# A decoder layer on one core: transpositions written into the out-projection's row parts, a gain row spread first on TensorE, and the last sums of one gate block held back

## The chip, the core and the metric

The kernel runs on one core of a Trainium2 chip, in one launch. The metric is device time in microseconds. TensorE is called PE in the profile, and its weight loads PEld; VectorE is DVE, ScalarE is ACT, GpSimd is POOL and SyncE is SP. Every matrix product of the layer is done in three PE passes over a number that has been split into a high and a low part, so "H" and "L" at the end of a tile's name are the two halves of one operand.

## The reference

One layer of a hybrid decoder on 1024 tokens of width 1024, in float32:

```
h = rms_norm(x, norm_mix)
proj = h @ w_in                      # 1024 x 8192: xa, ga, q, f, v, g, m_a, m_b
y_a = rg_lru(conv(xa)) * gelu(ga)
y_b = rms_norm(hgrn2(silu(q), f, v), hg_norm) * silu(g)
y = sigmoid(m_a) * y_a + sigmoid(m_b) * y_b
x = x + y @ w_out                    # out-projection
h = rms_norm(x, norm_mlp)
x = x + square(relu(h @ w_up)) @ w_down
out = rms_norm(x, norm_final)
```

## The kernel before

**Stages.** The tokens are worked in two halves of 512 (`c` = 0, 1), each half in four row tiles of 128 tokens. In order of time: `first_norm` brings in the first four row tiles, normalises and transposes them; eight stages of projections and recurrences follow (to about 560 us); then the gate products (`gate_step`, `gate_work`); then the out-projection, for the first half in `out_proj(0, ...)` and for the second half in a loop over two "row parts" of two row tiles each; then the MLP's first product (`product`, `hidden`) and its second one, with the final norm at the end.

**What sets the order.** A scheduler orders each engine's instructions by priority and by its own estimate of when an operand is ready, except where `keep` or `pin` record that an instruction stays in the order of the source (`pin` only while `pinned[0]` is true), where `add_manual_dep(..., NoSync, ...)` puts one instruction behind another on the same engine, or where `high_priority` lifts it.

**The start.** `first_norm` (L281 on) loads x, weights, and the 1 x 1024 row of the first norm's gain (`gain_row`, on ACT's DMA queue). The gain is spread over 128 partitions by two matmuls of a row of ones (written by POOL, L298) with that row (L305), into two PSUM banks (`spread`). PE also runs transposes of an identity matrix into a bank that nobody reads (`idle`): five ahead of the two matmuls (L302) and seven behind them (L307). ACT copies the two halves of the spread gain to SBUF (L335), DVE scales the first row tile by them (L328), PE transposes it (L178), ACT casts the high half (`hT00H`, L87), and the first projection (`pv`) begins.

**The gates.** There are sixteen gate blocks `q`; block q % 4 says which of the four gate kinds it is, and the four blocks of a channel pair are combined into `y`. Blocks 0 and 1 were made earlier, so `own` is the list 2 to 15: `own[0]` = 2, `own[1]` = 3, `own[2]` = 4. A block has seven products of 12 matmuls each (steps 0 to 6 of `PLAN`, a Strassen-like scheme); steps 0, 2, 4 and 6 add into one bank X. Steps 0, 1 and 2 are copied out by ACT; steps 3, 4 and 5 are added up by DVE (L1071); step 6 is copied out by ACT (L1073). Step 6 adds on to the bank that step 4's DVE addition reads. In the profile a block's operands carry its number plus 32: `wA1236` is step 3's and 6's weight of block 4. `gate_work(3)` finishes the first `y`: a product with g1 (L1121), four sums with g2 (L1124), and the split into `yH` (ACT) and `yL` (DVE). It stands in the source behind all seven steps of block 3, as every block's work does. The block's first product and the next block's are placed by the scheduler there.

**The out-projection.** `out_proj(0, ...)` runs 192 matmuls (8 weight tiles x 2 x 4 row tiles x 3 passes) and adds x (L929). `second_norm(tt, 0)` for the four row tiles then does: sum of squares on ACT (L165), rstd on DVE and POOL (L166, L171), scaling on DVE (L172), eight PE transposes into two "hg" banks (L1268), a copy of each bank by ACT (L1269) and the split of it. The row parts (`for part in range(2)`) follow: each has two halves `hf` of the output columns, each half four weight tiles `j`, each of them 12 matmuls (2 x 2 row tiles x 3 passes) in the bank `po`. The transposes of the first half's four tiles (`xT_h`) have been issued in the source ahead of this loop, and those of the second half's tiles at the end of their row part; where they stand on PE among the loop's matmuls is the scheduler's choice, since `pinned[0]` is set only in the last quarter (part 1, hf 1). `second_norm(tt, 1)` ends in `operands()`, a generator of the MLP's combined operands (t1, B22, n2, T3, T4), on DVE and ACT, run by `rest_of_it`.

Of the kernel before, what the change touches and what calls it, by code (L numbers as in the profile page):

```python
# [18 lines left out]
P = 128  # L19
# [26 lines left out]
def trunk(ctx: ExitStack, tc: tile.TileContext, x, wts, mlp, pv, gains, mask_f, mask_u, out):  # L46
# [236 lines left out]
    def first_norm():  # L283
        dst = hT[0]
        halves = (slice(0, D // 2), slice(D // 2, D))
        xts = []
        for tt in range(4):
            xt = mt(X_TAGS[tt], f"x{tt}", (P, D))
            for cols in halves if tt == 0 else (slice(0, D),):
                nc.sync.dma_start(xt[:, cols], x[tt * P : (tt + 1) * P, cols])  # L290
            xts.append(xt)
            if tt < 2:
                raws.append(load_w(tt))
        raws.append(load_w(2))
        line = mt("qb", "gain_row", (P, 1792))
        row, ones = line[0:1, 0:D], line[0:1, D : D + P]
        nc.scalar.dma_start(row, gains[0:1, :])
        G.memset(ones, 1.0)  # L298
        gain0.append(const.tile([P, D], F32, tag="gain", name="gain0", bufs=1))
        idle = bank("sc", "idle")  # L300
        for _ in range(5):
            keep(PE.transpose(idle[:, :P], ident, ident))  # L302
        spread = [bank("pj", f"gain{h}") for h in range(2)]
        for h, cols in enumerate(halves):
            keep(PE.matmul(spread[h], ones, row[:, cols], start=True, stop=True))  # L305
        for _ in range(7):
            keep(PE.transpose(idle[:, :P], ident, ident))  # L307
        xns, rs = {}, {}

        def squares(tt):  # L310
            xn = xns[tt] = mt("f" if tt % 2 == 0 else "tmp", f"xn0{tt}", (P, D))
            r = rs[tt] = const.tile([P, 1], F32, tag="rstd", name=f"rstd_x0{tt}", bufs=4)
            if tt:
                keep(A.activation(xn, xts[tt], AF.Square, scale=D**-0.5, accum_out=r))
                keep(V.tensor_scalar(r, r, EPS, None, op0=ALU.add))
            else:
                two = const.tile([P, 2], F32, tag="ossq", name="first_sq", bufs=8)
                for h, cols in enumerate(halves):
                    keep(A.activation(xn[:, cols], xts[tt][:, cols], AF.Square, scale=D**-0.5, accum_out=two[:, h : h + 1]))
                keep(V.tensor_tensor(out=r, in0=two[:, 0:1], in1=two[:, 1:2], op=ALU.add))  # L320
                keep(V.tensor_scalar(r, r, EPS, None, op0=ALU.add))
            keep(G.tensor_tensor(out=r, in0=r, in1=mhalf[:, 0:1], op=ALU.pow))

        def scaled(tt):
            for h, cols in enumerate(halves) if tt == 0 else ((0, slice(0, D)),):
                g = gain0[0][:, cols] if tt else spread[h]
                keep(
                    V.scalar_tensor_tensor(  # L328
                        xns[tt][:, cols], xts[tt][:, cols], rs[tt][:, 0:1], g, op0=ALU.mult, op1=ALU.mult
                    )  # L330
                )

        squares(0)
        for h, cols in enumerate(halves):
            keep(A.copy(gain0[0][:, cols], spread[h]))  # L335
        scaled(0)
        fill_w(1)
        squares(1)
        for tt in range(4):
            transposed(xns[tt], dst, tt, f"x0{tt}")  # L340
            if tt < 3:
                scaled(tt + 1)
                if tt < 2:
                    squares(tt + 2)
                if tt == 0:
                    fill_w(2)
        fill_w(3)
        in_order[0] = False
# [735 lines left out]
    def gate_work(q):  # L1084
# [28 lines left out]
        else:  # L1113
# [3 lines left out]
            for c in range(NC):  # L1117
                two = slice(2 * c, 2 * c + 2)
                for j in (2 * c, 2 * c + 1):
                    A.activation(b[:, j, :], b[:, j, :], AF.Sigmoid, scale=SIGN[j])  # L1120
                V.tensor_tensor(out=b[:, two, :], in0=b[:, two, :], in1=g1[:, two, :], op=ALU.mult)  # L1121
                for j in (2 * c, 2 * c + 1):
                    op = ALU.add if p == 0 or SIGN[j] > 0 else ALU.subtract
                    V.tensor_tensor(out=b[:, j, :], in0=b[:, j, :], in1=g2[:, j, :], op=op)  # L1124
                if last and c == 0:
                    split(b[:, two, :], yt[0][p][:, 0], yt[0][p][:, 1])
                else:
                    split(b[:, two, :], yh[:, two, :], yl[:, two, :])
                    for t, y in enumerate((yh, yl)):
                        nc.sync.dma_start(yd[p][:, t, two, :], y[:, two, :].bitcast(F32))  # L1130
# [51 lines left out]
    for q in own:  # L1182
# [3 lines left out]
        for step in (1, 2, 5, 4, 6) if q == own[0] else (0, 1, 2, 3, 4, 5, 6):  # L1186
# [3 lines left out]
            gate_step(q, step)  # L1190
            if q == own[0] and step == 4:
                gate_step(own[1], 0)
            if q == own[1] and step == 6:
                pinned[0] = False
                gate_step(own[2], 0)
                with_o(0)
                gate_work(own[0])
# [13 lines left out]
            for k in {2: ("sums", "a", "b"), 5: ("c",), 6: ("d",)}.get(step, ()):  # L1211
                if q > own[0]:
                    gwork[n][k]()
                elif k != "a":
                    with tc.high_priority(300):
                        gwork[n][k]()
        if q > own[0]:
            gate_work(q)
    close_gp()
    close_tp()  # L1220
# [32 lines left out]
    def second_norm(tt, half):  # L1253
# [8 lines left out]
        def op_split(src, o):  # L1262
            return split(src.rearrange("p (k t) -> p k t", k=4), hop[o][0][:, :, cut], hop[o][1][:, :, cut])

        for h in range(2):
            pt = bank("hg", f"xT_h{t}_{h}")
            for k in range(4):
                pin(PE.transpose(pt[:, k * P : (k + 1) * P], xn[:, (4 * h + k) * P : (4 * h + k + 1) * P], ident))  # L1268
            A.copy(b[:, h, :], pt)  # L1269
            if half == 0:  # L1270
                op_split(b[:, h, :], ("B11", "B21")[h])

        def operands():
            b0 = braw[tt, 0]
# [18 lines left out]
            op_split(b21, "T4")  # L1293
            yield

        return operands()

    rest, t1_ops, n2_ops = [], [], []

# [26 lines left out]
                work[0]["sums"]()  # L1326
                work[0]["b"]()

    for tt in range(4):
        second_norm(tt, 0)  # L1330
    close_rows()
    homes("B22")
    for part in range(2):
        tts = (2 * part, 2 * part + 1)
        for tt in tts:
# [2 lines left out]
        for hf in range(2):  # L1338
            pp = {tt: bank("pj", f"po1{hf}{tt}") for tt in tts}
            turn = [(j, tts) for j in range(4)]  # L1340
            if (part, hf) == (1, 1):
                turn = turn[:2] + [(j, tts[i : i + 1]) for i in range(2) for j in (2, 3)]
                pinned[0] = True
            for n, (j, those) in enumerate(turn):
                if n == 4:
                    first_weights()
                wh, wl = out_w[4 * hf + j]
                for k in range(2):
                    ku = 2 * j + k
                    yh, yl = ykt1(part, ku)  # L1350
                    cols = slice(k * 512, (k + 1) * 512)
                    for tt in those:
                        cut = slice((tt % 2) * P, (tt % 2 + 1) * P)
                        mm3(pp[tt], yh[:, cut], yl[:, cut], wh[:, cols], wl[:, cols], ku == 0, ku == 7)
            for tt in tts:
                cols = slice(hf * 512, (hf + 1) * 512)
                V.tensor_tensor(out=x2s[tt][:, cols], in0=pp[tt], in1=x2s[tt][:, cols], op=ALU.add)
        for i, tt in enumerate(tts):
            if part:
                product(i, 0)  # L1360
            nc.sync.dma_start(x2d[4 + tt], x2s[tt])
            rest.append(second_norm(tt, 1))
    with tc.high_priority(400):
        work[0]["d"]()
    product(0, 3)
# [270 lines left out]
```

## Time and profile before

| | us |
|---|---|
| runs: median of 3 | 1549.08 |
| runs: lowest, highest | 1548.0, 1550.54 |
| the profiled execution's own time | 1550.47 |
| its span, first to last instruction | 1548.7 |
| PE busy | 1528.6 (99%) |
| PEld busy | 1274.5 (82%) |
| DVE busy | 1151.0 (74%) |
| ACT busy | 809.3 (52%) |
| POOL busy | 154.5 (10%) |

A line of the timeline gives start, duration, engine, source line, operation, output<-inputs, shapes and a count where neighbours of one kind were merged; a bracket at its end gives how long the engine had been idle before it, and what ended that. A line of the waits gives who waited for whom, the total, how often, and the longest. Matmuls are pipelined: the time from one start to the next is what one costs, and it is shorter than the duration shown.

### The profile page before, as it was taken

What the parts mean: (1) busy time and instruction counts of PE and PEld (TensorE: products, weight loads), DVE (VectorE), ACT (ScalarE), POOL (GpSimd) and SP (SyncE); (2) the same over time, 40 slices, a digit from 0 to 9 for tenths busy, and PEclk for the clock granted to TensorE, in tenths of its full rate; (3) what the DMA queues carried; (4) which work ended last, traced back from release to release, by engine and by line L of the source; (5) the groups of instructions that cost most, each with busy time, mean ns of one, the idle gap of its engine ahead of it and who ended that gap; (6) DMA issues with size and microseconds to landing.
All of it is one profiled execution on the core that took longest, in us unless ns stands there. A gap on an engine that the chain in (4) does not pass through costs nothing. (4 is left out here: it accounts for less than half of the span.)

```text
span 1548.7 us, 23204 instructions
## 1 busy us (share of the span) xinstructions
PE 1528.6 (99%) x9088; PEld 1274.5 (82%) x9088; DVE 1151.0 (74%) x1656; ACT 809.3 (52%) x1341; POOL 154.5 (10%) x188
## 2 busy tenths in 40 slices
PE   9999999999999999999999999999999999999998
PEld 7878888888888887888888778888888788888886
DVE  5798695485675838786856568888888898888877
ACT  5656757567567335454533347766776721111115
POOL 1022210232614600000000000000000000000000
PEclk9999999999999999999999999999999999999999
DMA  8545455465674275332339223666666675666642
GB/s 295 191 158 191 150 192 195 150 215 173 222 229 140 99 295 187 126 136 82 136 107 333 117 109 141 268 246 250 248 251 247 220 307 215 253 250 251 253 187 109
DMA packets 81679, 306.82 MB, mean 198 GB/s; under 512 B 8481, under 2 KB 20897, under 8 KB 68642
## 3 DMA queue, kind: packets, MB, share of 16 engines
q1 hardware_dynamic: 77536, 292.75, 51.5%
q10 hardware_dynamic: 4034, 12.59, 2.1%
q8 instruction: 71, 1.16, 0.3%
q14 instruction: 38, 0.31, 0.1%
HBM read 201.50 MB, written 103.81 MB: 197 GB/s over the span
## 5 line engine op out<-in xcount | busy, mean ns | idle before, releaser
L1545 DVE TENSOR_TENSOR acc<-acc,dX 128x512 f32<-128x512 f32 x128 | 85.2, 685 | 28.8 <-PE dX L146 27.2
L87 ACT CAST wA<-q 128x512 fp32r<-128x512 f32 x46 | 28.6, 622 | 148.3 <-PE dX L146 102.4
L88 DVE TENSOR_TENSOR wL<-raw,wH 128x1024 fp32r<-128x1024 f32 x48 | 58.9, 1226 | 43.1 <-ACT wH L87 42.8
L87 ACT CAST wH<-raw 128x1024 fp32r<-128x1024 f32 x48 | 50.4, 1050 | 36.7 <-DMA raw<-wts_in 14.5
L1545 DVE TENSOR_TENSOR acc<-acc,dY 128x512 f32<-128x512 f32 x64 | 43.5, 686 | 13.1 <-PE dY L146 12.9
L145 PE MATMUL po<-wL,y 128*128 128x512 f32 x128 | 50.0, 391 | 0.0
L146 PE MATMUL po<-wH,y 128*128 128x512 f32 x128 | 49.9, 391 | 0.0
L144 PE MATMUL po<-wH,y 128*128 128x512 f32 x128 | 49.5, 390 | 0.0
L1406 ACT ACTIVATE b<-b 128x512 f32<-128x512 f32 x48 | 30.2, 630 | 32.7 <-DVE b L1405 32.5
L88 DVE TENSOR_TENSOR wA<-q,wA 128x512 fp32r<-128x512 f32 x46 | 31.5, 687 | 19.0 <-ACT wA L87 18.9
L108 ACT CAST wH<-raw 128x1024 fp32r<-128x1024 f32 x36 | 37.7, 1048 | 9.7 <-issue 3.7
L171 POOL TENSOR_TENSOR rstd_h<-rstd_h,mhalf 128x1 f32<-128x1 f32 x8 | 4.6, 585 | 376.1 <-DVE rstd_h L166 376.1
L465 DVE SCALAR_TENSOR_TENSOR xc<-xp,pvt,xc 128x512 f32<-128x512 f32 x48 | 40.1, 846 | 1.1 <-ACT xc L449 1.1
L981 DVE TENSOR_TENSOR s<-q,q 128x512 f32<-128x512 f32 x46 | 31.6, 688 | 5.3 <-DMA q<-mlp_in 5.0
L378 POOL TENSOR_TENSOR stt<-r,stt 128x256 fp32r<-128x256 f32 x16 | 19.8, 1261 | 127.4 <-ACT stt L377 115.3
L989 DVE TENSOR_TENSOR s<-q 128x512 f32<-128x512 f32 x46 | 31.6, 687 | 0.4
L1407 ACT ACTIVATE b<-b 128x512 f32<-128x512 f32 x48 | 30.2, 631 | 1.2
L769 ACT ACTIVATE on<-po 128x128 f32<-128x128 f32 x64 | 16.9, 278 | 26.1 <-PE po L765 26.0
L144 PEld LDWEIGHTS po<-wH,y 128*128 128x128 f32 x128 | 24.0, 188 | 4.9
L145 PEld LDWEIGHTS po<-wL,y 128*128 128x128 f32 x128 | 24.0, 188 | 4.9
L146 PEld LDWEIGHTS po<-wH,y 128*128 128x128 f32 x128 | 24.0, 188 | 4.8
L1071 DVE TENSOR_TENSOR gb<-gY,ge 128x512 f32<-128x512 f32 x14 | 9.7, 691 | 24.1 <-PE gY L146 24.1
(2548 smaller groups left out, 5453.6 us busy)
## 6 DMA issues: line engine op xcount, KB each, us to landing
q<-mlp_in SPq DMA_DIRECT2D x92, 512.0 KB, 3.7
raw<-wts_in SPq DMA_DIRECT2D x80, 512.0 KB, 4.8
rest<-wL SPq DMA_DIRECT2D x36, 512.0 KB, 2.9
wL<-rest SPq DMA_DIRECT2D x36, 512.0 KB, 4.1
hd<-ri SPq DMA_DIRECT2D x16, 256.0 KB, 3.8
od<-onT ACTq DMA_DIRECT2D x8, 512.0 KB, 7.1
cdT<-stT SPq DMA_DIRECT2D x16, 256.0 KB, 3.2
o<-od SPq DMA_DIRECT2D x4, 1024.0 KB, 7.4
```

Source lines behind the costliest of these rows:

```text
L87: keep(A.copy(h, src))
L88: ins = V.tensor_tensor(out=lo, in0=src, in1=h.bitcast(F32), op=ALU.subtract)
L108: A.copy(h, raw)
L144: pin(PE.matmul(o, ah, bh, start=first, stop=False, **how))
L145: pin(PE.matmul(o, ah, bl, start=False, stop=False, **how))
L146: pin(PE.matmul(o, al, bh, start=False, stop=last, **how))
L465: ins = V.scalar_tensor_tensor(xc[:, s, :], xp[:, j : j + T], pvt[:, PV_CW + 8 * j + u : PV_CW + 8 * j + u + 1], xc[:, s, :], op0=ALU.mult ...
L981: ins = V.tensor_tensor(out=sa[:, 0, :], in0=a21, in1=a22, op=ALU.add)
L989: V.tensor_tensor(out=sb[:, 0, :], in0=a21, in1=a11, op=ALU.add)
L1406: A.activation(b[:, at, :], b[:, at, :], AF.Relu, scale=-1.0 if at == 2 else 1.0)
L1407: A.activation(b[:, at, :], b[:, at, :], AF.Square)
L1545: V.tensor_tensor(out=dst, in0=dst, in1=banks[bk, pr], op=op)
```

## The change

Three places are edited.

**Start.** The five idle transposes ahead of the two gain matmuls go, and of the seven behind them five stay. On PE the program began, before:

```order
L302 MATMUL idle<-ident 128x128 x5
L305 MATMUL gain_156<-gain_row 128x512
L305 MATMUL gain_157<-gain_row 128x512
L307 MATMUL idle<-ident 128x128 x7
L178 MATMUL xT_x_0_190<-ident,xn_167 128x128 x4
L178 MATMUL xT_x_1_197<-ident,xn_167 128x128 x4
```

and begins now:

```order
L305 MATMUL gain_151<-gain_row 128x512
L305 MATMUL gain_152<-gain_row 128x512
L307 MATMUL idle<-ident 128x128 x5
L178 MATMUL xT_x_0_183<-ident,xn_160 128x128 x4
L178 MATMUL xT_x_1_190<-ident,xn_160 128x128 x4
```

The gain matmuls are now PE's first instructions. They no longer stand behind the identity matrix.

**Gates.** `gate_work(3)` is issued after step 4 of block 4 instead of after block 3, and its sums L1124 get an order (no semaphore) behind block 4's step-4 addition. On DVE, around the end of the first `y` (`gb_6351` is block 3's sum, `gb_6487` is block 4's), before:

```order
L88 TENSOR_TENSOR ws137L<-s_6573,ws137H 128x1024
L1121 TENSOR_TENSOR gb_6351<-gb_6351,gb_6246 128x1024 x2
L1124 TENSOR_TENSOR gb_6351<-gb_6351,g_0_6279 128x512 x4
L88 TENSOR_TENSOR yL_6521<-gb_6351,yH_6520 128x1024
L1071 TENSOR_TENSOR gb_6487<-gZ_6586,ge_4_6500 128x512
L1071 TENSOR_TENSOR gb_6487<-gX_6486,ge_4_6553 128x512
```

and now (`gb_6344` is block 3's, `gb_6480` is block 4's):

```order
L88 TENSOR_TENSOR ws137L<-s_6546,ws137H 128x1024
L1071 TENSOR_TENSOR gb_6480<-gZ_6559,ge_4_6493 128x512
L1121 TENSOR_TENSOR gb_6344<-gb_6344,gb_6239 128x1024 x2
L1071 TENSOR_TENSOR gb_6480<-gX_6479,ge_4_6526 128x512
L1124 TENSOR_TENSOR gb_6344<-gb_6344,g_0_6272 128x512 x4
L1071 TENSOR_TENSOR gb_6480<-gY_6513,ge_4_6544 128x512
L88 TENSOR_TENSOR yL_6587<-gb_6344,yH_6586 128x1024 x2
```

Block 4's three additions now stand between and ahead of block 3's last sums. On PE the 12 matmuls of block 4's step 6 (`gX<-gT4H,wA1236H` and its fellows) stood behind the 12 of block 5's step 0 and one of its step 1; now they stand ahead of them. The split `wA` of block 6's first weight moves a few places back on DVE, and on SP one weight load (`q<-mlp_in`) moves ahead of the load `o<-od`.

**Out-projection.** In `second_norm` the transposes with their copies and splits become a function `turned()` that the caller runs. The four of the first half are run after chosen weight tiles of part 0 (hf 0 after the second, third and fourth; hf 1 after the first), those of part 0's own tiles after the second and third of part 1, and those of part 1's tiles where they were. `pinned[0]` is true from the start of the loop. On PE, around the first of these transposes, before (11 matmuls of part 0 stand ahead):

```order
L145 MATMUL po_8538<-wL_8051,y_8150 128x512
L146 MATMUL po_8538<-wH_8050,y_8150 128x512
L144 MATMUL po_8539<-wH_8050,y_8150 128x512
L145 MATMUL po_8539<-wL_8051,y_8150 128x512
L1268 MATMUL xT_h_0_8446<-ident,xn_h_8440 128x128 x4
L1268 MATMUL xT_h_1_8454<-ident,xn_h_8440 128x128 x4
L146 MATMUL po_8539<-wH_8050,y_8150 128x512
L144 MATMUL po_8538<-wH_8096,y_8151 128x512
L145 MATMUL po_8538<-wL_8097,y_8151 128x512
L1268 MATMUL xT_h_0_8468<-ident,xn_h_8462 128x128 x4
```

and now (24 matmuls of part 0 stand ahead, and 12 between each two groups of transposes):

```order
L144 MATMUL po_8468<-wH_8089,y_8144 128x512
L145 MATMUL po_8468<-wL_8090,y_8144 128x512
L146 MATMUL po_8468<-wH_8089,y_8144 128x512
L1274 MATMUL xT_h_0_8493<-ident,xn_h_8433 128x128 x4
L1274 MATMUL xT_h_1_8501<-ident,xn_h_8433 128x128 x4
L144 MATMUL po_8467<-wH_8095,y_8145 128x512
L145 MATMUL po_8467<-wL_8096,y_8145 128x512
L146 MATMUL po_8467<-wH_8095,y_8145 128x512
```

The groups of the first half stood after 11, 14, 18 and 22 matmuls of the loop and stand now after 24, 36, 48 and 60; the two of part 0's tiles move from 13 and 15 matmuls into part 1 to 24 and 36. Before, several groups split a row of three passes.

The diff:

```diff
@@ first_norm
-        for _ in range(5):
+        for _ in range(0):
             keep(PE.transpose(idle[:, :P], ident, ident))
         spread = [bank("pj", f"gain{h}") for h in range(2)]
         for h, cols in enumerate(halves):
             keep(PE.matmul(spread[h], ones, row[:, cols], start=True, stop=True))
-        for _ in range(7):
+        for _ in range(5):
             keep(PE.transpose(idle[:, :P], ident, ident))
@@ gate_work
                     op = ALU.add if p == 0 or SIGN[j] > 0 else ALU.subtract
-                    V.tensor_tensor(out=b[:, j, :], in0=b[:, j, :], in1=g2[:, j, :], op=op)
+                    ins = V.tensor_tensor(out=b[:, j, :], in0=b[:, j, :], in1=g2[:, j, :], op=op)
+                    if q == own[1]:
+                        how = mybir.DependencyInfo(mybir.DependencyClass.NoSync, mybir.DependencyReason.DATA)
+                        tc.add_manual_dep(ins.ins, added[own[2], 4].ins.name, how, reason="sums of the next")
@@ the loop over the blocks
+            if q == own[2] and step == 4:
+                gate_work(own[1])
...
-        if q > own[0]:
+        if q > own[1]:
             gate_work(q)
@@ second_norm
-        for h in range(2):
-            pt = bank("hg", f"xT_h{t}_{h}")
-            for k in range(4):
-                pin(PE.transpose(pt[:, k * P : (k + 1) * P], xn[:, (4 * h + k) * P : (4 * h + k + 1) * P], ident))
-            A.copy(b[:, h, :], pt)
-            if half == 0:
-                op_split(b[:, h, :], ("B11", "B21")[h])
+        def turned():
+            for h in range(2):
+                pt = bank("hg", f"xT_h{t}_{h}")
+                for k in range(4):
+                    pin(PE.transpose(pt[:, k * P : (k + 1) * P], xn[:, (4 * h + k) * P : (4 * h + k + 1) * P], ident))
+                A.copy(b[:, h, :], pt)
+                if half == 0:
+                    op_split(b[:, h, :], ("B11", "B21")[h])
...
-        return operands()
+        return turned, operands()
@@ the row parts
-    for tt in range(4):
-        second_norm(tt, 0)
+    turns = {}
+    for tt, at in enumerate(((0, 0, 1), (0, 0, 2), (0, 0, 3), (0, 1, 0))):
+        turns[at], _ = second_norm(tt, 0)
     close_rows()
     homes("B22")
+    pinned[0] = True
...
             if (part, hf) == (1, 1):
                 turn = turn[:2] + [(j, tts[i : i + 1]) for i in range(2) for j in (2, 3)]
-                pinned[0] = True
...
+                if (part, hf, n) in turns:
+                    turns.pop((part, hf, n))()
...
-            rest.append(second_norm(tt, 1))
+            turn, ops = second_norm(tt, 1)
+            rest.append(ops)
+            if part:
+                turn()
+            else:
+                turns[1, 0, i + 1] = turn
```

## The prediction

> **What bounds the kernel now.** I read the page first, then the waits by PE, then the timeline at each edited place. The page says that PE is the bound:
>
> ```profile
> PE 1528.6 (99%) x9088; PEld 1274.5 (82%) x9088; DVE 1151.0 (74%) x1656; ACT 809.3 (52%) x1341; POOL 154.5 (10%) x188
> ```
>
> PE does the same products after the change, so only its stalls can be won: the span of 1548.7 us less 1528.6 busy leaves 20.1 us, much of which is the short gap at each change of operands. The waits by PE name the larger stalls of which the change speaks:
>
> ```profile
> PE gX L144 <- DVE gb L1071: 1.2, 1, 1.2
> PE xT_h L1268 <- DVE xn_h L172: 0.9, 2, 0.5
> PE xT_h L1268 <- ACT ws10H L87: 0.7, 1, 0.7
> PE xT_h L1268 <- ACT h2B11H L87: 0.6, 1, 0.6
> PE xT_h L1268 <- DVE rstd_h L166: 0.3, 1, 0.3
> ```
>
> The first is a gate product; the other four lines are five stalls at the transposes of the out-projection. The idle time understates a stall, since PE is still shown busy while its pipeline drains; I count from start to start below. The first ten microseconds are a third place: there PE is shown busy with transposes that nobody reads.
>
> **The out-projection.** Two neighbours give the normal step; then come the five stalled groups, the last start before the fourth group, the start of part 1, and the scaling of the fourth row tile:
>
> ```profile
> 872.59 0.39 PE L144 MATMUL po<-wH,y 128*128 128x512 f32 x1
> 872.82 0.39 PE L145 MATMUL po<-wL,y 128*128 128x512 f32 x1
> 873.51 1.09 PE L1268 MATMUL xT_h<-ident,xn_h 128*128 128x128 f32 x8 [0.30 <-DVE rstd_h L166]
> ...
> 875.62 1.06 PE L1268 MATMUL xT_h<-ident,xn_h 128*128 128x128 f32 x8 [0.32 <-DVE xn_h L172]
> ...
> 879.01 0.39 PE L144 MATMUL po<-wH,y 128*128 128x512 f32 x1
> 880.03 1.06 PE L1268 MATMUL xT_h<-ident,xn_h 128*128 128x128 f32 x8 [0.62 <-ACT h2B11H L87]
> ```
>
> ```profile
> 897.76 0.39 PE L144 MATMUL po<-wH,y 128*128 128x512 f32 x1
> ...
> 901.55 1.06 PE L1268 MATMUL xT_h<-ident,xn_h 128*128 128x128 f32 x8 [0.68 <-ACT ws10H L87]
> ...
> 903.62 1.06 PE L1268 MATMUL xT_h<-ident,xn_h 128*128 128x128 f32 x8 [0.54 <-DVE xn_h L172]
> ```
>
> A step is 0.23 us. From 872.82 to 873.51 is 0.69, so the first stall costs 0.46 with an idle of 0.30: the drain adds 0.16 to each. The fourth group: 880.03 - 879.01 - 0.23 = 0.79, again 0.17 over its idle of 0.62. The five together: idle 0.30 + 0.32 + 0.62 + 0.68 + 0.54 = 2.46, plus 5 x 0.16 = 3.3 us.
>
> Is the operand there at the new places? The eleventh matmul of the loop starts at 872.82, so the first did at 872.82 - 10 x 0.23 = 870.5. With 24 ahead the first group comes at 870.5 + 5.5 = 876.0; its rows were used at 873.51, a margin of 2.5 us. Each next group comes 12 steps and a group later, 2.75 + 0.9: 879.7, 883.3, 887.0; before, the second came at 875.62 and the fourth at 880.03. The two banks are free long before, since ACT takes 0.59 for such a copy (in the start's rows below), 1.2 for a group's two, and there are 2.75 between groups. In part 1, from 897.76 on, the groups come at 903.3 and 907.0 on the old clock, against 901.55 and 903.62. So all five stalls go. The new pins add nothing by themselves: `po` matmuls stood in that order before, only with groups pushed in among them. Bounds: 3.3 is all there is, plus nothing; at the low end I leave half a stall, 0.4, at each of the two groups of part 1, whose ACT queue now has two weight casts ahead of the copies: 2.5. I take **3.3**.
>
> What is late next is DVE's work behind the second pair's transposes; one weight split in it, its end, and what follows:
>
> ```profile
> 903.39 1.22 DVE L88 TENSOR_TENSOR ws10L<-s,ws10H 128x1024 fp32r<-128x1024 f32 x1
> ...
> 917.17 0.69 DVE L1290 SCALAR_TENSOR_TENSOR xn_h<-xn_h,xn_h 128x512 f32<-128x512 f32 x1
> 920.40 0.69 DVE L1357 TENSOR_TENSOR x2s<-po,x2s 128x512 f32<-128x512 f32 x1 [2.53 <-PE po L146]
> ```
>
> It has 2.53 us to spare ahead of the last sums of the out-projection, which PE brings 3.3 us earlier; the queue of DVE itself starts 1.7 earlier (the first three stalls, 0.46 + 0.48 + 0.79). So 2.53 - (3.3 - 1.7) = 0.9 us remain, if DVE finds other work while it waits for the later groups; three weight splits of 1.2 us each (`ws10L`, `wA120L`, `ws30L`) are there for it.
>
> **The gate block.** PE at block 5's step 0 and at the stall, then DVE:
>
> ```profile
> 613.36 0.39 PE L144 MATMUL gX<-hT00H,wA 128*128 128x512 f32 x1
> ...
> 616.08 0.39 PE L144 MATMUL gY<-gt1H,ws137H 128*128 128x512 f32 x1
> 617.66 0.50 PE L144 MATMUL gX<-gT4H,wA1236H 128*128 128x512 f32 x1 [1.20 <-DVE gb L1071]
> ```
>
> ```profile
> 610.45 2.36 DVE L1121 TENSOR_TENSOR gb<-gb,gb 128x1024 f32<-128x1024 f32 x2
> 612.72 2.50 DVE L1124 TENSOR_TENSOR gb<-gb,g 128x512 f32<-128x512 f32 x4
> 615.18 1.23 DVE L88 TENSOR_TENSOR yL<-gb,yH 128x1024 fp32r<-128x1024 f32 x1
> 616.33 0.68 DVE L1071 TENSOR_TENSOR gb<-gZ,ge 128x512 f32<-128x512 f32 x1
> 616.93 0.68 DVE L1071 TENSOR_TENSOR gb<-gX,ge 128x512 f32<-128x512 f32 x1
> ```
>
> The stall is 617.66 - 616.08 - 0.23 = 1.35 us: step 6 adds on to the bank that the last addition shown reads, and DVE reaches it only at 616.93 because the sums and one split stand ahead. Now DVE goes from 610.45: addition of gZ (616.93 - 616.33 = 0.60 a step) to 611.05, the two products (612.72 - 610.45 = 2.27) to 613.32, addition of gX done at 613.32 + 0.68 = 614.00. PE, which has step 6 next instead of step 0 of block 5, is ready at 613.36 and starts at 614.05: a stall of 0.7 remains, **0.7** is won. That the sums are held costs DVE nothing, since it has the same instructions; the sums start 613.92 - 612.72 = 1.2 us later and the splits `yL` follow. Behind them wait the stores of y and, on SP, the load `o<-od` into the same buffer; block 5's work reads it after that block's 84 products, 84 x 0.23 = 19 us of cover. The weight load moved ahead of it on SP is for block 7, which is still further off; without that cover a late o or weight would cost PE its lateness one to one. Bounds: 0 if DVE is held elsewhere and PE then stalls as long at the earlier place, 1.35 if the order leaves no stall.
>
> **The start.**
>
> ```profile
> q10 hardware_dynamic: 2, 0.00, 0.5%
> ```
>
> ```profile
> 2.26 0.20 POOL L298 MEMSET gain_row<- 1x128 f32 x1
> ...
> 2.37 1.33 PE L302 MATMUL idle<-ident 128*128 128x128 f32 x5 [2.37 <-POOL ident masks.py:199]
> ...
> 3.63 3.78 PE L305 MATMUL gain<-gain_row 1*128 1x512 f32 x4
> ...
> 7.33 1.76 PE L307 MATMUL idle<-ident 128*128 128x128 f32 x7
> 7.44 0.59 ACT L335 COPY gain<-gain 128x512 f32<-128x512 f32 x1 [1.12 <-PE gain L305]
> ...
> 8.06 0.75 DVE L328 SCALAR_TENSOR_TENSOR xn<-x,rstd_x,gain 128x512 f32<-128x512 f32 x1 [0.62 <-ACT gain L335]
> ...
> 8.87 1.06 ACT L314 ACTIVATE xn<-x 128x1024 f32<-128x1024 f32 x1
> 8.88 1.91 PE L178 MATMUL xT_x<-ident,xn 128*128 128x128 f32 x8
> ...
> 9.98 0.59 ACT L87 CAST hT00H<-xT_x 128x512 fp32r<-128x512 f32 x1
> ...
> 10.62 0.58 PE L144 MATMUL pv<-wH,hT00H 128*128 128x256 f32 x1
> ...
> 13.68 1.03 PE L178 MATMUL xT_x<-ident,xn 128*128 128x128 f32 x8
> ```
>
> The first line is from the DMA view of the first 2 us: both packets of ACT's queue, the gain row and its signal, are through by then. The ones are written at 2.46, so the gain matmuls can start at 2.5 instead of 3.63: 1.1 us. They end at 6.3; the five idle transposes (0.25 each) at 7.5; the second half of the first tile, which waited 0.62 for the copy, is scaled from 7.44 on. Transposes run from 7.5 instead of 8.88. On ACT the squares of the next tile stand ahead of `hT00H`:
>
> ```profile
> L290 SPq DMA_DIRECT2D x<-x_in x1: 432/432/432, 2.1 to 2.1; - x1
> ...
> DMA to landing us min/median/max: 5.8/5.8/5.8
> ```
>
> That tile lands at 2.1 + 5.8 = 7.9, so the squares move from 8.87 to no earlier than 7.9, and the cast from 9.98 to about 9.1. I take **0.9**, which the rest of the start (same engines, same order, the same queue of loads) hands on. Bounds: 1.1 above; below, the clock. The eight transposes at 8.88 take 1.91 and the same eight at 13.68 take 1.03: PE runs at about half pace until some point between, although it is shown busy from 2.37. The granted clock in the profile stands at full there and does not show it. If the idle transposes help to bring the full pace on, leaving out seven (1.8 us of PE work) could delay it by that much, which at half pace costs 0.9: the low end is 0.
>
> The Trainium skill, "TensorE: Matmul & The Clock Gate", Part 1, says that the array leaves half clock after a busy window of about 3.4 us; by that alone the gain matmuls would suffice, and the trace, with eight busy microseconds at half pace, disagrees. Its Part 4 says that transposes do not count as busy for this gate; by that rule the seven lost ones cost nothing and the term stays at 0.9, and the trace agrees as far as it shows.
>
> **The sum** is 3.3 + 0.7 + 0.9 = 4.9 us. The profiled execution took 1550.47, of which 1548.7 is span; it becomes 1545.6. That execution is 1.39 above the median of the runs, 1549.08, which becomes **1544.2**.
>
> **Rivals.** (1) The pace of PE comes later, without the transposes. For it: the half pace above. Against it: PE stays busy from 2.5 on without a gap. If the turn came one whole group of first products late, 3.4 us at half pace, the start would lose 1.7 - 0.9 = 0.8 instead of winning 0.9: 1549.08 - 4.0 + 0.8 = 1545.9. (2) The transposes' stalls only move: DVE, late with the second pair, hands the 3.3 us back at the MLP's first products. For it: the slack of 0.9. Against it: work to fill in. 1549.08 - 1.6 = 1547.5. (3) Slower. A pinned PE waits wherever a group is not ready, with all the matmuls behind it. Suppose ACT, in order, holds the copies of one group behind a weight cast that needs PE to be further on: then the next group finds no bank, PE and DVE both stand still, and each microsecond beyond the 0.9 goes to the end. It becomes slower from a delay of 0.9 + 4.9 = 5.8 us; two weight tiles of 2.75 with a group each, 7.3 us, give 1549.08 - 4.9 + 7.3 - 0.9 = 1550.6. Against it: the waits show `ws10H` released by PE after one weight tile, and the next casts need the following ones, each ahead of its group. (4) The hold does not do what it says, and step 6 stalls as before: 1544.9, within the forecast.
>
> **The numbers.** Forecast, with (4): 0.73. (1): 0.12. (2): 0.09. (3): 0.06. A measurement of this kernel tells about 0.2%, 3.1 us, from no change. The forecast is faster by 4.9; (1) by 3.2, which is on the edge, so two thirds of it count as faster; (2) is the same. Faster 0.73 + 0.08 = 0.81, same 0.04 + 0.09 = 0.13, slower 0.06. The forecast's bounds are 2.5 + 0 + 0 at the least and 3.3 + 1.35 + 1.1 = 5.75 at the most; the runs shown scatter by 1 us. The range goes from 1542.6, a little beyond the most, to 1547.4, at the least of the forecast and nearly at (2).
>
> **What would show it.** Right: in the waits by PE no line of xT_h with a stall ahead of the row parts' `uX`; one wait of about 0.5 idle at `gX<-gT4H,wA1236H`; gain matmuls at 2.5 and the first `pv` near 9.7. Wrong: gain matmuls at 2.5 but `pv` not earlier, transposes at half pace beyond 13 us, a stall of over a microsecond between 903 and 945, or `x2s` sums of part 1 that DVE begins long after their last `po`.

## The result, and the profile after

| | us | runs |
|---|---|---|
| before, same chip | 1550.3 (1548.0 to 1551.7) | 6 |
| after | 1544.12 (1543.3 to 1546.03) | 6 |
| ratio | 0.9968, 95% interval 0.9957 to 0.9978 | |
| profiled execution after | 1546.03, span 1544.2 | 1 |

The forecast was 1544.2, faster, and the whole interval lies below 1. At 1550 us the ratio is 5.0 us less, 3.4 to 6.7. The profiled execution is the slowest of the six.

The page's first part, after: the engine, its busy time with its share of the span, its instructions.

```profile
span 1544.2 us, 23190 instructions
PE 1527.6 (99%) x9081; PEld 1275.3 (83%) x9081; DVE 1150.0 (74%) x1656; ACT 810.2 (52%) x1341; POOL 149.8 (10%) x188
```

PE has seven instructions less, the idle transposes, and its busy time fell by 1.0 us; the other 3.5 of the 4.5 us by which the span is shorter are idle time. The waits by PE (who waited for whom: total, times, longest), after:

```profile
PE gain L305 <- DMA gain_row<-gains_in: 2.7, 1, 2.7
PE pv L144 <- ACT hT00H L87: 1.6, 1, 1.6
...
PE gX L144 <- DVE gb L1071: 0.4, 1, 0.4
```

No line of `xT_h` is left, and the gate's wait fell from 1.2 to 0.4. But there is a new one of 1.6 at the first `pv` product. The three places one by one, in PE's timeline after:

```profile
876.16 0.39 PE L145 MATMUL po<-wL,y 128*128 128x512 f32 x1
876.38 0.40 PE L146 MATMUL po<-wH,y 128*128 128x512 f32 x1
876.62 1.04 PE L1274 MATMUL xT_h<-ident,xn_h 128*128 128x128 f32 x8
877.41 0.48 PE L144 MATMUL po<-wH,y 128*128 128x512 f32 x1
...
901.99 1.03 PE L1274 MATMUL xT_h<-ident,xn_h 128*128 128x128 f32 x8
...
905.60 1.03 PE L1274 MATMUL xT_h<-ident,xn_h 128*128 128x128 f32 x8
```

The first group starts 0.24 us after the product ahead of it, a normal step, and no group has a bracket: all five stalls are gone. DVE's last sums of the out-projection still have time to spare in DVE's timeline after:

```profile
917.57 0.69 DVE L1366 TENSOR_TENSOR x2s<-po,x2s 128x512 f32<-128x512 f32 x1 [1.09 <-PE po L146]
```

DVE waited 1.09 us for PE there, against 2.53 before and 0.9 forecast. The gate block after, PE and then DVE:

```profile
614.50 0.39 PE L146 MATMUL gY<-hT11H,ws336L 128*128 128x512 f32 x1
615.31 0.50 PE L144 MATMUL gX<-gT4H,wA1236H 128*128 128x512 f32 x1 [0.42 <-DVE gb L1071]
```

```profile
612.31 2.34 DVE L1121 TENSOR_TENSOR gb<-gb,gb 128x1024 f32<-128x1024 f32 x2
614.58 0.68 DVE L1071 TENSOR_TENSOR gb<-gX,ge 128x512 f32<-128x512 f32 x1
615.18 2.48 DVE L1124 TENSOR_TENSOR gb<-gb,g 128x512 f32<-128x512 f32 x4
```

The addition of `gX` now stands ahead of the sums, and the stall is 615.31 - 614.50 - 0.23 = 0.58 us, against 1.35. The start after, PE and then ACT:

```profile
7.51 1.91 PE L178 MATMUL xT_x<-ident,xn 128*128 128x128 f32 x8
11.08 0.58 PE L144 MATMUL pv<-wH,hT00H 128*128 128x256 f32 x1 [1.65 <-ACT hT00H L87]
...
14.46 1.91 PE L178 MATMUL xT_x<-ident,xn 128*128 128x128 f32 x8
...
17.17 0.28 PE L145 MATMUL pv<-wL,hT01H 128*128 128x256 f32 x1
```

```profile
8.15 1.05 ACT L87 CAST wH<-raw 128x1024 fp32r<-128x1024 f32 x1 [1.07 <-DMA raw<-wts_in]
9.40 1.06 ACT L314 ACTIVATE xn<-x 128x1024 f32<-128x1024 f32 x1 [0.21 <-DMA x<-x_in]
10.37 0.19 ACT L314 ACTIVATION_READ_ACCUMULATOR xn<-x 128x1 f32 x1
10.46 0.57 ACT L87 CAST hT00H<-xT_x 128x512 fp32r<-128x512 f32 x1
```

The gain matmuls start at 2.7, where 2.5 was forecast: PE waited there for the load of the gain row, which the forecast had taken to be through within the first 2 us. The transposes start at 7.51, 1.4 earlier than before, as forecast. But the first `pv` product comes at 11.08, not at 9.7 and later than the 10.62 of before, and PE's full pace (products 0.12 apart instead of 0.21) comes near 17 instead of 12.4. ACT's two brackets say why: it waited for the loads of the first weight tile and of the second row tile, and the cast `hT00H` stands behind both.

An account of the two spans, 4.5 us apart. PE's first block of scores over 64 columns starts at 99.68 before and 101.31 after: +1.6. The out-projection: -3.3. The gate block: -0.8. What is left is about -2.0, and nearly all of it lies where nothing was edited: PE's stalls of over a quarter of a microsecond behind 945 us come to 3.2 before and 1.3 after, by the spacing of its products. So two edits gave what was forecast, the third gave nothing here, and a difference that is not the change's stands in its place. The experiments take these apart.

### The profile page after: what moved, and what is told of

It reads as the page before. It is cut to its first block, busy times and chain, and to the rows that moved or that the text cites. A ratio compares the mean times of both kernels' runs of the same rounds, so it can differ in the third digit from the quotient of the medians.

```text
span 1544.2 us, 23190 instructions
## 1 busy us (share of the span) xinstructions
PE 1527.6 (99%) x9081; PEld 1275.3 (83%) x9081; DVE 1150.0 (74%) x1656; ACT 810.2 (52%) x1341; POOL 149.8 (10%) x188
## 5 line engine op out<-in xcount | busy, mean ns | idle before, releaser
L1559 DVE TENSOR_TENSOR acc<-acc,dY 128x512 f32<-128x512 f32 x64 | 43.4, 685 | 13.1 <-PE dY L146 12.9
```

Source lines behind the costliest of these rows:

```text
L1559: V.tensor_tensor(out=dst, in0=dst, in1=banks[bk, pr], op=op)
```

## The experiments

### One edit at a time

Each of the first three runs has one edit of the diff shown above on the kernel before, with the other two left out; the fourth is the changed kernel with the start of before:

```diff
-        for _ in range(0):
+        for _ in range(5):
             keep(PE.transpose(idle[:, :P], ident, ident))
...
-        for _ in range(5):
+        for _ in range(7):
             keep(PE.transpose(idle[:, :P], ident, ident))
```

> The kernel before with the start's edit alone. My theory (the start moves earlier by up to 0.9 us when the loads land as before, and landing times are chance): gain matmuls at 2.5 to 2.8 us, first pv product between 9.5 and 11.2 depending on when the second row tile lands, the transposes of the second tile at half pace or full by chance; time 0 to 1 us under the kernel before. Rival A (seven transposes fewer bring PE's full pace on a few us later): transposes of the second row tile at half pace (1.9 us for eight) again and full pace only after 15 us, time 1 to 2 us over the kernel before.

> The kernel before with the held sums of the first y alone. My theory: the stall of 1.35 us at step 6 of gate block 4 shrinks to 0.6 to 0.7, nothing else moves; time 0.7 us under the kernel before, which is below what the rounds tell. Rival B (the delay of y and of the loads behind it comes back in a later block): a new stall of PE of 0.3 us or more between 620 and 700 us, time equal to the kernel before or longer.

> The kernel before with the transposes written into the row parts alone. My theory: all five stalls at the transposes go and PE gets from the first row-part product to the MLP's first product 3.3 us sooner, with no new stall over 0.3 us up to 945 us; time 3.3 us under the kernel before. Rival C (half of the measured gain is from the stretch 1215 to 1280 us, where stalls of 2.2 us vanished in the changed kernel because its rows are in another phase to the loads): the same stalls vanish here, time 5 us or more under. If they stand as in the kernel before, or come and go without the edit, they are chance of the loads' landing.

> The changed kernel with the start of the kernel before (five idle transposes ahead, seven behind). My theory (the start is worth nothing to 0.9 us): 4 us under the kernel before, equal to or up to 0.9 us over the changed kernel. Rival A (the new start costs 1 to 2 us because PE's full pace comes late): 5.5 to 6 us under the kernel before, full pace by 12.5 us in its profile.

| | median us | runs | ratio to before, 95% interval |
|---|---|---|---|
| before | 1549.5 | 33 | |
| start alone | 1549.43 | 11 | 0.9998, 0.9989 to 1.0007 |
| gate alone | 1548.62 | 11 | 0.9997, 0.9988 to 1.0006 |
| out-projection alone | 1545.96 | 11 | 0.9982, 0.9973 to 0.9991 |
| without the start | 1546.31 | 11 | 0.9981, 0.9972 to 0.9989 |

The out-projection's edit alone makes the kernel measurably faster. PE's waits in its profile have no line of `xT_h`; in the profile of the gate's edit alone all five stalls are there still:

```profile
PE xT_h L1273 <- DVE xn_h L172: 1.2, 3, 0.5
PE xT_h L1273 <- ACT ws10H L87: 0.7, 1, 0.7
PE xT_h L1273 <- ACT h2B11H L87: 0.6, 1, 0.6
```

The gate's edit works as meant, but the stall that it shortens was not always 1.35. PE's row with the out-projection's edit alone, so with the old gate order, and with the gate's edit alone:

```profile
616.61 0.50 PE L144 MATMUL gX<-gT4H,wA1236H 128*128 128x512 f32 x1 [0.76 <-DVE gb L1071]
```

```profile
614.28 0.50 PE L144 MATMUL gX<-gT4H,wA1236H 128*128 128x512 f32 x1 [0.55 <-DVE gb L1071]
```

From start to start these are 0.93 and 0.71. Over the three profiles with the old order the stall is 1.35, 0.93 and 0.83; over the nine with the change's order 0.27 to 0.71, 0.54 in the mean. The edit is worth about 0.5 us, which medians of these runs cannot show.

The late stalls are not the change's. The three of 0.7 to 1.0 us that the profile before has at 1232.6, 1248.5 and 1279.2 are absent in the profile of the start's edit alone, which touches nothing near them (it has one of 1.5 at 1033.5 instead). Two variants of the change below have one of 1.2 at 1244.7 and one of 0.7 at 1242.7 again.

### The start

Alone, the start's edit changed nothing that the medians show, and the profiles have the first `pv` product between 10.2 and 11.1. Two causes were in question: PE's pace, and the loads. The next three kernels move or drop the idle transposes of the changed kernel. The first adds five behind the first row tile's transposes, the second also takes the other five away, the third has none:

```diff
             transposed(xns[tt], dst, tt, f"x0{tt}")
+            for _ in range(5 if tt == 0 else 0):
+                keep(PE.transpose(idle[:, :P], ident, ident))
```

```diff
-        for _ in range(5):
-            keep(PE.transpose(idle[:, :P], ident, ident))
```

> The changed kernel with five more idle transposes behind the first row tile's transposes, so that TensorE has no gap between those and the first pv product (the changed kernel's profile showed a gap of 1.65 us there, the kernel with the new start alone 0.66). Theory gap: TensorE's full pace comes 2.8 to 6.8 us after it has become busy without a gap with 128-row work; here that is at about 6.3 to 6.5, so the turn comes at 9.3 to 13.5 us, against 14.47 and 17.17 with the gap, and the score products (sc64) start at 99.3 to 100.0 us if the loads land as early as before (101.28 and 100.0 with the gap). Rival, count: the turn follows the number of transposes put in, wherever they stand; ten against twelve of the old start gives a turn like the old start's, 10.1 to 14.0. Rival, chance: the turn has nothing to do with either and lies anywhere from 10 to 17 us. Time: within 0.1% of the changed kernel.

> The changed kernel with its five idle transposes moved from behind the gain matmuls to behind the first row tile's transposes: the same number, in another place. Theory gap: TensorE now pauses between the gain matmuls (end about 6.3) and the first tile's transposes (8 to 9.4), but not behind them, so the count starts with those transposes at 8 to 9.4 and the turn comes at 11 to 15 us, mostly ahead of the changed kernel's 17.17. Rival, count: five transposes as in the changed kernel, so the turn stays at 14.5 to 17.2 us.

> The changed kernel with no idle transposes at all. Theory gap: the five transposes behind the gain matmuls bring nothing, since the gap behind the first tile's own transposes starts the count again; the first pv starts where it did (10.2 to 11.1) and the turn comes 2.8 to 6.8 us behind it, 13.5 to 17.5 us, as in the two profiles with the new start. Rival, count: five transposes fewer delay the turn by at least their 1.25 us against those two, to 15.7 to 18.5 us. The rule of the Trainium skill that transposes do not count gives the same as the first.

The first gave 1544.06 (10 runs, ratio 0.997, 0.996 to 0.9979), the other two, in one run each, 1544.28 and 1543.78. Then the change and the change without its start ran once more, on one chip:

> The changed kernel once more, on one chip with the next run, which has the old start and the other two edits. Theory: the new start is worth 0 to 0.3 us, since the loads bound the second half of the start; the two medians then differ by less than 1 us. Rival: the start is worth the 0.9 us predicted or more once the other edits are in (the medians of separate chips, 1544.12 against 1546.31, would say 2.2): this run is then 0.9 to 2.2 us below the next. In the profile, by the theory: the first pv product starts 1.65 to 1.70 us after the load of the second row tile has landed, or at 9.6 to 9.7 us if that is before 8.0.

> The changed kernel with the start of the kernel before, once more. Theory: within 1 us of the run of the changed kernel on the same chip; rival: 0.9 to 2.2 us above it. In the profile, by the theory: the first pv product starts at 10.62 us, whenever the second row tile lands before 8.9, and 1.65 to 1.70 us after that landing otherwise.

They gave 1544.74 (7 runs; ratio 0.9974, 0.9963 to 0.9984) and 1545.38 (11 runs; 0.9978, 0.9969 to 0.9987). Here is the start of every profile, in order of the landing of the second row tile's load; "full pace" is when PE's steps turn short:

| | second row tile landed | first `pv` | full pace about | scores over 64 columns |
|---|---|---|---|---|
| *old start:* out-projection alone | 7.82 | 10.62 | 10.1 | 99.39 |
| before | 7.92 | 10.62 | 12.4 | 99.68 |
| gate alone | 8.79 | 10.62 | 11.9 | 99.96 |
| without the start | 9.06 | 10.76 | 13.4 | 100.37 |
| the same again | 9.24 | 10.94 | 12.9 | 100.62 |
| *new start:* no idle transposes | 7.91 | 9.60 | 11.3 | 99.49 |
| ten idle transposes | 8.47 | 10.30 | 11.2 | 100.04 |
| start alone | 8.52 | 10.22 | 14.5 | 100.03 |
| products held (below) | 8.87 | 10.56 | 13.7 | 100.09 |
| the change again | 8.94 | 10.64 | before 10.6 | 100.12 |
| five, moved | 9.07 | 10.77 | 15.9 | 100.82 |
| after | 9.38 | 11.08 | 17.0 | 101.31 |

With the new start the first `pv` product comes 1.69 or 1.70 us after that landing in every row (ten idle transposes, which PE itself had to finish, make it 1.83). With the old start it comes at 10.62, or 1.70 after the landing if that is later: in the rows of the prediction ACT's copy of the gain waits for PE's gain matmuls until 7.44, so ACT comes to the squares only at 8.87; and PE, at half pace, is through with its transposes at about 10.6 too. ACT's rows without idle transposes show the chain in an execution with an early landing, and PE's the effect:

```profile
7.93 1.06 ACT L312 ACTIVATE xn<-x 128x1024 f32<-128x1024 f32 x1
8.89 0.19 ACT L312 ACTIVATION_READ_ACCUMULATOR xn<-x 128x1 f32 x1
8.98 0.56 ACT L87 CAST hT00H<-xT_x 128x512 fp32r<-128x512 f32 x1
```

```profile
9.60 0.58 PE L144 MATMUL pv<-wH,hT00H 128*128 128x256 f32 x1
```

That is the 9.7 of the forecast, which had taken the landing of the profile before, 7.9. Most executions land later, with either start.

To try the landing as the cause, ACT's squares of the second row tile were put behind the two casts:

```diff
         fill_w(1)
-        squares(1)
         for tt in range(4):
             transposed(xns[tt], dst, tt, f"x0{tt}")
+            if tt == 0:
+                squares(1)
```

> The changed kernel with ScalarE's squares of the second row tile put behind the two casts of the first tile's transposes, so that the cast hT00H, for which the first pv product waits, no longer stands behind the landing of that row tile. Theory (the landing sets the first pv product): it now starts less than 1.3 us after that landing, 0.5 to 1.0 us earlier than by the rule of 1.65 to 1.70, and is set by the landing and cast of the first weight tile instead; the score products (sc64) do not start more than 0.3 us earlier than in a look with equal landings, since the loads bound the second half of the start. Rival (something else, such as TensorE's pace or the transposes, sets it): it stays 1.65 to 1.70 us behind the landing, or at 10.2 or later. Time: within 0.1% of the changed kernel.

It gave 1544.5 (8 runs, ratio 0.9976, 0.9966 to 0.9986). The tile landed at 8.53; by the rule `pv` would come at 10.22. PE's timeline:

```profile
9.66 0.58 PE L144 MATMUL pv<-wH,hT00H 128*128 128x256 f32 x1
...
13.79 1.94 PE L178 MATMUL xT_x<-ident,xn 128*128 128x128 f32 x8 [0.91 <-DVE rstd_x L315]
```

It comes 1.13 after the landing, 0.56 earlier than by the rule, so the landing set it through ACT's order. What sets it now is not the cast of the first weight tile, as expected, but the transposes, which run at half pace from 7.87 on; ACT waits 0.68 for them ahead of `hT00H`. And it is worth nothing: the next row tile's transposes now wait 0.91, and the scores start at 100.58, against 100.03 for nearly the same landing in the run with the start alone. Part of that can be the late turn to full pace, which came near 17.2 here.

Even an early first product is lost by 100 us. Without idle transposes `pv` starts 1.02 earlier than before with the same landing (7.91 and 7.92), the second row tile's transposes 0.82, the third's 0.84, the fourth's 0.25, the scores 0.2. Between the third and the fourth stand ACT's squares of the fifth row tile. Their row before, their row without idle transposes, and then PE's wait that follows in the latter:

```profile
16.33 1.06 ACT L165 ACTIVATE xn<-x 128x1024 f32<-128x1024 f32 x1
```

```profile
16.34 1.06 ACT L165 ACTIVATE xn<-x 128x1024 f32<-128x1024 f32 x1 [0.73 <-DMA x<-x_in]
```

```profile
20.35 0.38 PE L146 MATMUL pv<-wH,hT00L 128*128 128x256 f32 x1 [0.67 <-DVE hT00L L88]
```

Before, ACT came to them at 16.33 straight from other work; without idle transposes it was there 0.73 earlier and waited for the load, to 16.34. DVE scales that tile ahead of the split `hT00L`, and PE waits 0.67 for the split. Fitted by a straight line over the twelve rows of the table and the run without transposes that follows below (8.70, 100.24), the scores start 0.9 us later for each microsecond of landing, and the new start makes 0.1 later, with a standard error of 0.14.

The theory of the gap was that PE comes to full pace 2.8 to 6.8 us after it has become busy without a pause on 128-row work. A profile that seems to contradict it is the change run again; PE's rows:

```profile
7.36 1.91 PE L178 MATMUL xT_x<-ident,xn 128*128 128x128 f32 x8
10.64 0.38 PE L144 MATMUL pv<-wH,hT00H 128*128 128x256 f32 x1 [1.37 <-ACT hT00H L87]
10.86 0.28 PE L145 MATMUL pv<-wL,hT00H 128*128 128x256 f32 x1
```

PE stood still for 1.37 us, and the very first product has the 0.38 of full pace (0.58 in the first profile of the change). Of the theory's forecasts for the three kernels, two failed. Ten transposes (11.2) turned where both the theory and its rival, the count of transposes, said. But five in the gap gave 15.9, beyond the 11 to 15 that the theory forecast, and none at all gave 11.3, earlier than either allowed: the number does not set it.

The theory is not refuted by this, though. The two forecasts had assumed where the pauses would be, and the profiles have them elsewhere. With the five moved, one was left ahead of `pv`, and without idle transposes, with the early landing, there was none:

```profile
10.77 0.58 PE L144 MATMUL pv<-wH,hT00H 128*128 128x256 f32 x1 [0.22 <-ACT hT00H L87]
```

Counted from the end of the last pause that the timeline marks ahead of the turn, or else from the first 128-row work behind the gain matmuls, the turn comes 2.8 to 6.1 us later in thirteen of the fourteen profiles. The fourteenth, the change run again, fits if the turn came at the end of the transposes or in the pause. What counts as a pause was chosen here after the fact, and no run tests it: what sets the turn stays open.

The old start turned between 10.1 and 13.4 in five profiles. Of the eight with five idle transposes or none, six turned at 13.7 or later. That the idle transposes, or the pause that they fill, make a late turn rarer would fit this, but so few profiles do not show it. A late turn seems to cost a little: from the change run again to its first profile the scores are 1.19 later, of which the landing, 0.44 later, makes 0.4. With the time of the turn as a further term (10.6 for the change run again, 15 for the last run below), the fit over thirteen profiles gives 0.10 us later scores for each microsecond of a later turn (standard error 0.03), 0.7 for each of landing, and nothing for the new start itself.

### The stall that is left in the gate block

DVE's two products ahead of the addition take 2.27 us and are as little needed there as the sums:

```diff
-                V.tensor_tensor(out=b[:, two, :], in0=b[:, two, :], in1=g1[:, two, :], op=ALU.mult)
+                ins = V.tensor_tensor(out=b[:, two, :], in0=b[:, two, :], in1=g1[:, two, :], op=ALU.mult)
+                if q == own[1]:
+                    how = mybir.DependencyInfo(mybir.DependencyClass.NoSync, mybir.DependencyReason.DATA)
+                    tc.add_manual_dep(ins.ins, added[own[2], 4].ins.name, how, reason="products of the next")
```

> The changed kernel with the second gate block's last two products held behind the addition of gX too (the change holds only the sums). Theory: the stall left at step 6 (0.58 us from start to start, idle 0.42) is DVE's two products ahead of that addition, 2.27 us; without them DVE ends the addition 2.27 us earlier, ahead of the end of PE's step before it, and the stall is 0. Gain 0.6 us, 0.04%, which the rounds cannot tell: ratio to the kernel before 0.996 to 0.998, like the changed kernel. Rival: what is held back comes late further on: the split yL, the addition of gY or the next block's gate work gives a new stall of 0.3 us or more between 612 and 645.

It gave 1544.45 (7 runs, ratio 0.9972, 0.9962 to 0.9983). DVE's timeline and PE's:

```profile
610.74 0.68 DVE L1071 TENSOR_TENSOR gb<-gX,ge 128x512 f32<-128x512 f32 x1
611.34 2.35 DVE L1121 TENSOR_TENSOR gb<-gb,gb 128x1024 f32<-128x1024 f32 x2
```

```profile
612.82 0.39 PE L146 MATMUL gY<-hT11H,ws336L 128*128 128x512 f32 x1
613.04 0.39 PE L144 MATMUL gX<-gT4H,wA1236H 128*128 128x512 f32 x1
```

The step from one product to the next is 0.22: the stall is gone, and none stands between there and 645. The time did not show it, since this profile lost 4.0 us behind 945. The largest stall, 2.0 at 1029.5, stands behind a weight load for which ACT waited:

```profile
1025.45 0.62 ACT L87 CAST wA<-q 128x512 fp32r<-128x512 f32 x1 [3.38 <-DMA q<-mlp_in]
```

The next, 1.2 at 1244.7, follows an addition by DVE; its row in this profile, and the same addition before:

```profile
1242.81 0.69 DVE L1562 TENSOR_TENSOR acc<-acc,dX 128x512 f32<-128x512 f32 x1 [1.73 <-DMA acc<-x]
```

```profile
1246.58 0.69 DVE L1545 TENSOR_TENSOR acc<-acc,dX 128x512 f32<-128x512 f32 x1 [1.21 <-DMA acc<-x]
```

A load into `acc` came late, by more here than before the change. Over the fourteen profiles PE's stalls behind 945 come to between 0.7 (three of them) and 4.0 us, with no order by kernel. The last run joins this edit to the start without idle transposes:

> The changed kernel without its five idle transposes and with the second gate block's last two products held behind the addition of gX as well as the sums: the shortest form that keeps the stalls out. Theory: no stall at step 6 of the gate block (0.5 to 0.6 us less), the start as in the other looks with the new start: 0.5 us below the changed kernel, which five rounds can hardly tell. Rival: without the transposes TensorE's full pace comes late when the loads land late, and the start gives the 0.6 us back: equal to the changed kernel or up to 1 us above it.

It gave 1544.92 (9 runs, 1542.16 to 1546.53; ratio 0.9973, 0.9963 to 0.9982). The gate's stall is absent again; `pv` started at 10.39 and PE reached full pace near 15. Neither this nor the other variants can be told from the change, so no version was found that beats it.

## Why the prediction was right, and where it was not

**Out-projection, 3.3.** Right. All five stalls go, 3.3 us by the spacing of the products, and alone the edit gives 3.5 between medians (by its ratio 2.8, 1.4 to 4.2). Rival (2), the stall handed on to the MLP's first products, did not occur: 1.09 of DVE's slack is left, 0.9 was forecast. Nor did rival (3): no pinned group waits.

**Gate block, 0.7.** The mechanism and the stall that remains (0.7 forecast, 0.58 in the profile after) are right; the size was a little high, since the 1.35 of the profile before was the largest of three. About 0.5 was there to win. Rival (4), that the hold does nothing, is out by the order on DVE.

**Start, 0.9.** This step failed. "That tile lands at 2.1 + 5.8 = 7.9, so the squares move from 8.87 to no earlier than 7.9" was the right chain with one execution's landing in it. With the old start ACT, held up by PE's gain matmuls, came to the squares only at 8.87, which hid any earlier landing; with the new one each later landing goes in full into the first `pv`, and the landings shown run from 7.8 to 9.4. Then "which the rest of the start [...] hands on" was wrong even with an early landing: the fifth row tile's load takes back most of it, and 0.2 arrives. In the profiles the start is worth nothing within 0.3 us. Between medians it is 0.1 alone, and the changed kernel against itself with the old start gives, from the two pairs of ratios, 0.0013 and 0.0004, or 2.0 and 0.6 us, where each ratio is good to 0.001. So by the runs' times a worth of 1 us is not excluded, though no profile shows one; that is not settled.

Two of the forecast's own signs of being wrong showed in the profile after: `pv` not earlier, and transposes at half pace beyond 13 us (at 14.46). The second is the sign of rival (1), full pace late. The ground held against that rival, that PE stays busy from 2.5 on without a gap, did not hold: PE paused for 1.65 ahead of `pv`. The rival's price of 1.7 did not come: the late turn cost some 0.8 there by one comparison, 0.6 by the fit, and in the next profile of the same kernel it was gone. What sets the turn stays open. On one point the traces say more. The Trainium skill, "TensorE: Matmul & The Clock Gate", Part 4, says that transposes do not count as busy for the clock gate in the way that other matmuls do. In PE's rows of the out-projection's edit alone

```profile
6.34 1.06 PE L305 MATMUL gain<-gain_row 1*128 1x512 f32 x1
7.33 1.75 PE L307 MATMUL idle<-ident 128*128 128x128 f32 x7
8.88 1.62 PE L178 MATMUL xT_x<-ident,xn 128*128 128x128 f32 x8
10.62 0.39 PE L144 MATMUL pv<-wH,hT00H 128*128 128x256 f32 x1
```

the eight transposes take 1.62, between the 1.91 of half pace and the 1.03 of full pace, and the first product has full pace: the turn came among transposes, with nothing else on PE since the one-row gain matmuls ended at 7.4. The trace disagrees with the rule, unless those matmuls alone brought the turn on, some 2.7 us after their end.

**The sum.** 4.9 was forecast. The single edits give 0.1 + 0.9 + 3.5 = 4.5 between medians, and 0.3 + 0.5 + 2.8 = 3.6 by their ratios; the change gave 5.0 (3.4 to 6.7) and, again, 4.0 (2.5 to 5.7). In the two profiled executions the difference of 4.5 is made of -3.3, -0.8, +1.6 and about -2.0, nearly all of it from late stalls that are not the change's. The forecast of the time came out, but in part by luck: 0.9 of its 4.9 was not there, the interval cannot tell 4.0 from 4.9, and in the profiled pair fewer late stalls made up for it. The range has a slip: its slow end, 1547.4, is called the least of the forecast, but 2.5 off 1549.08 is 1546.6.

## What to carry to other kernels

A stall of PE at work that can stand anywhere, such as transposes whose operands come from another engine, is removed whole by writing that work down later, as long as the engine that makes the next operands has slack left: read that slack off its longest wait. Earlier work at a kernel's start is worth what the next load allows: before counting it, follow the chain to the first row that waits for a DMA, and take landings from several executions, not one. And a term below the scatter of late stalls (here 0.7 to 4.0 us between executions of one design) is read from its own place in the trace, never from the total.

## What was not expected of the hardware

The load of one row tile, issued at 2.1 to 2.4 us in each, landed anywhere from 7.8 to 9.4 us in kernels with the same loads, and no edit explains which. PE's step from half to full pace came anywhere between 10.1 and 17.2 us; in one execution a pause of 1.37 us ended at full pace, and in another the step came among transposes, ahead of the first projection. The profile's granted clock shows nothing of it: it reads 1.00 there in every profile. And the largest unforced difference between two executions was not at the start but in single stalls behind 945 us, the largest of them behind loads: 3.3 us between the best and the worst of fourteen profiles.
